# Block 1 of a feed-forward up-projection: two weight sums written over the raw gate weights, and the gate vector of the feed-forward asked for in blocks 8 to 15

## The chip, the cores and the metric

The kernel runs on one core of a Trainium2 chip. The metric is the device time of one execution in microseconds (us); lower is better. Engines: PE is TensorE (matrix products), DVE is VectorE, ACT is ScalarE, POOL is GpSimd, and SP is SyncE, whose queue issues most of the DMAs.

## What is computed

One layer of a diffusion transformer on 1024 positions of width 1024, all in fp32: a Hyena mixer, then a convolutional feed-forward with 2816 hidden channels. The change lies in the feed-forward. Cut to what matters:

```python
def conv_ffn(u, w_up, conv_w, conv_b, w_down, rows, cols):
    a, g = jnp.split(u @ w_up, 2, axis=-1)
    g = grid_dwconv(g, conv_w, conv_b, rows, cols)      # 3 x 3, depthwise, on a 16 x 64 grid
    return (jax.nn.silu(g) * a) @ w_down

sh1, sc1, g1, sh2, sc2, g2 = adaln_params(c, mod_w, mod_b)
x = x + g1 * hyena_mix(modulate(rmsnorm(x, norm_g[0]), sh1, sc1), hy_params)
x = x + g2 * conv_ffn(modulate(rmsnorm(x, norm_g[1]), sh2, sc2), *ffn_p, rows, 64)
return rmsnorm(x, final_g)
```

`g2` is the gate vector: one sixth (piece 5) of the product of `silu(c)` with `mod_w`. It is used only after the down-projection has begun to give results.

## The kernel before

Every fp32 product is made of three fp32r products: each operand is split into a high part (a copy by ACT, `..h`) and a low part (source minus high part, by DVE or POOL, `..l`), and `mm3` (L57 to L59) issues three matmuls.

The up-projection (`ffn_up`) runs over 22 blocks of 128 hidden channels. A block needs 128 columns of gate weights `g` and 128 of value weights `a`, 128 x 1024 each, which `up_load` brings in (L933) into two buffers with the tag `raw`. Block 0 is an ordinary product (`up_half`, 96 matmuls). Blocks 1 to 21 use Strassen's scheme in Winograd's form: 7 products of 12 matmuls each, 84 a block, from the quarters A11, A12 (in `g`), A22 (in `a`) and the sums S1 to S4 of them, against the same sums T1 to T4 of the activations. `up_prep(b)` makes the weights' operands: gh and gl from `g`; S1 and S2 in `s12` (POOL, L973 and L974), S3 and S4 in `s43` (POOL, L975 and L976); then the high and low parts (L962 and L963). `s12` lies in buffer x2 and `s43` in x3, but block 1's `s12` lies in another tile (`junk`).

Buffers x0 to x3 hold the tiles `braw` until then: the quarters B11 and B21 of the activations, from which `self.tsum` makes T1 to T4 (DVE subtractions L912, splits L62 and L63, the tiles tT1 to tT4). Block 1 is prepared, in program order, ahead of `tsum`; its `s43` has to wait until braw3 is no longer read.

In a block, PE runs S1 into the bank `uz`, S2 into `s`; ACT copies both into `pu` (L1065, L1067); then S4 goes on top of `uz`, which DVE adds into the convolution's padded tile (L1073), and S3 on top of `s`, which DVE adds into `at` (L1075); then comes the first product of the next block, and then A22 by T4 on top of the same `s`, once L1075 has read it. `up_tail` runs the convolution of the block before: one ACT instruction (L1005) and eight on DVE (`facc`, L1010), the SiLU (L1012), the product (L1013) and the store (L1014).

The gate vector is made by the generator `mod_gen(5)`: eight steps, each a DMA of 512 KB into the one buffer `mw` (L282) and one DVE instruction over 128 x 1024 (`macc`, L284 or L286); the last step also adds a bias (L308), and sums over the partitions on PE (four matmuls, L312). `ffn_up` asks for one step at the end of each block from 2 on, so in blocks 2 to 9.

The order of the instructions on each engine isn't the order of the program alone. A scheduler of the framework fixes it when the kernel is built: position in the program is priority, and an instruction of low priority goes ahead wherever, by the scheduler's own model of time, its engine has nothing ready of higher priority. On the chip each engine then runs its own list strictly in that order. SP's queue does too.

Of the kernel before, what the change touches and what calls it, by code (L numbers as in the profile page):

```python
# [13 lines left out]
ALU = mybir.AluOpType  # L14
# [4 lines left out]
D = 1024  # L19
# [28 lines left out]
class Kern:  # L48
# [903 lines left out]
    def up_prep(self, b):  # L952
        nc, op = self.nc, self.op
        if b >= NHT:
            return
        self.up_load(b)
        g, a = self.upraw.pop(b)
        lo, hi = slice(0, 512), slice(512, 1024)
        A = {}

        def hl(which, h, l, src, eng):
            nc.scalar.activation(out=h, in_=src, func=AF.Copy)  # L962
            eng.tensor_tensor(out=l, in0=src, in1=h.bitcast(F32), op=ALU.subtract)  # L963
            for i, w in enumerate(which):
                A[w] = h[:, i * 512:i * 512 + 512], l[:, i * 512:i * 512 + 512]

        gh = self.wp.tile([128, D], F32R, tag="wh", name=f"gh{b}", bufs=2)
        gl = self.wp.tile([128, D], F32R, tag="wl", name=f"gl{b}", bufs=2)
        hl(("A11", "A12"), gh, gl, g, nc.vector)
        s12 = self.xtile(2, [128, D], f"s12_{b}") if b > 1 else op.tile([128, D], F32, tag="junk", name="s12_1")  # L970
        s43 = self.xtile(3, [128, D], f"s43_{b}")
        tt = nc.gpsimd.tensor_tensor
        tt(out=s12[:, lo], in0=a[:, lo], in1=a[:, hi], op=ALU.add)  # L973
        tt(out=s12[:, hi], in0=s12[:, lo], in1=g[:, lo], op=ALU.subtract)  # L974
        tt(out=s43[:, hi], in0=g[:, lo], in1=a[:, lo], op=ALU.subtract)  # L975
        tt(out=s43[:, lo], in0=g[:, hi], in1=s12[:, hi], op=ALU.subtract)  # L976
        h, l = (op.tile([128, D], F32R, tag=f"xn{i}", name=f"s12{x}{b}") for i, x in enumerate("hl"))
        hl(("S1", "S2"), h, l, s12, nc.vector)
        h, l = (op.tile([128, D], F32R, tag=f"xn{2 + i}", name=f"s43{x}{b}") for i, x in enumerate("hl"))
        hl(("S4", "S3"), h, l, s43, nc.gpsimd)  # L980
        h, l = (op.tile([128, 512], F32R, tag=t, name=f"a22{x}{b}", bufs=2) for t, x in (("ot", "h"), ("nt", "l")))
        hl(("A22",), h, l, a[:, hi], nc.gpsimd)
        self.A[b] = A
# [33 lines left out]
    def ffn_up(self):  # L1017
        nc, op = self.nc, self.op
        pads = []
        for i in range(2):  # L1020
            p = op.tile([128, 1216], F32, name=f"fpad{i}", tag=f"fpad{i}")
            nc.gpsimd.memset(p, 0.0)
            pads.append(p[:, 0:18 * 66].rearrange("p (r c) -> p r c", r=18))
        s0, at, x = {}, {}, {}
        mods = self.mod_gen(5, None)
        at[0] = op.tile([128, D], F32, tag="macc", name="at0")

        def p1(b):
            s0[b] = self.bank("mm", f"s0_{b}")
            self.up_mm(b, s0[b], "A11", "11", True)  # L1030
            x[b] = self.bank("mm", f"ux{b}")
            nc.scalar.activation(out=x[b], in_=s0[b], func=AF.Copy)

        def p2(b):
            self.up_mm(b, x[b], "A12", "21")
            nc.scalar.activation(out=pads[b % 2][:, 1:9, 1:65], in_=x.pop(b).rearrange("p (r c) -> p r c", r=8), func=AF.Copy)

        def p4(b):
            self.up_mm(b, s0[b], "A22", "T4")
            nc.scalar.activation(out=at[b][:, 0:512], in_=s0.pop(b), func=AF.Copy)  # L1040

        self.up_half(pads[0], at[0], 0)
        self.up_prep(1)
        p1(1)
        p2(1)
        for k in sorted(self.tsum):
            self.tsum[k]()
        self.up_half(pads[0], at[0], 1)
        for b in range(1, NHT + 1):
            if b < NHT:  # L1050
                self.up_prep(b + 1)
                if b > 1:
                    p1(b)
            if b > 1:
                p4(b - 1)
            self.up_tail(b - 1, pads[(b - 1) % 2], at.pop(b - 1))
            if b == NHT:
                break
            pad = pads[b % 2]
            z = self.bank("mm", f"uz{b}")  # L1060
            pu = op.tile([128, 2, 512], F32, tag="junk", name=f"pu{b}")
            p5, u2 = pu[:, 0], pu[:, 1]
            at[b] = self.xtile(1, [128, D], f"at{b}") if b % 2 else op.tile([128, D], F32, tag="macc", name=f"at{b}")
            self.up_mm(b, z, "S1", "T1", True)
            nc.scalar.activation(out=p5, in_=z, func=AF.Copy)  # L1065
            self.up_mm(b, s0[b], "S2", "T2")
            nc.scalar.activation(out=u2, in_=s0[b], func=AF.Copy)  # L1067
            if b == NHT - 1:
                self.down_start()
            if b > 1:  # L1070
                p2(b)
            self.up_mm(b, z, "S4", "22")
            nc.vector.tensor_tensor(out=pad[:, 9:17, 1:65], in0=z.rearrange("p (r c) -> p r c", r=8), in1=u2.rearrange("p (r c) -> p r c", r=8), op=ALU.add)  # L1073
            self.up_mm(b, s0[b], "S3", "T3")
            nc.vector.tensor_tensor(out=at[b][:, 512:1024], in0=s0[b], in1=p5, op=ALU.add)  # L1075
            if b >= 2:
                next(mods, None)

    def down_start(self):
# [395 lines left out]
```

## Time and profile before

| | us |
|---|---|
| median of 3 executions | 1323.33 |
| lowest, highest | 1321.83, 1326.72 |
| the profiled execution | 1323.98 |
| its span, first to last instruction | 1321.9 |
| PE busy in the span | 1241.8 |
| DVE busy in the span | 1071.6 |
| POOL busy in the span | 405.9 |

Times in the rows are us from the start of the span. PE's clock is given as a share of full speed: 1.0 is 2.4 GHz and half of it 1.2 GHz. The up-projection runs from about 606 us to about 1065 us of the span, and block 1 from about 637 us to 680 us. The stretch is read first by busy time, then by what PE waited for, then instruction by instruction.

### The profile page before, as it was taken

Reading aid. Unit: us, or ns where it says so; the run is one execution under the profiler, and the core shown is the slowest. Engines: PE = TensorE matmul, PEld = TensorE weight load, DVE = VectorE, ACT = ScalarE, POOL = GpSimd, SP = SyncE. Lnnn points to the kernel's source line nnn. Section 1 sums busy time; section 2 is a strip of 40 time slices with the busy share of each in tenths; the row PEclk is TensorE's granted clock in tenths of the full one; section 3 lists DMA queues with packets and bytes.
Section 4 is the critical chain, followed back from the end, with each engine's and each line's share of the span. In section 5 each row is a group of like instructions: output and inputs, shape, how many; then the busy total and the mean of one; then the engine's idle time right before and its main releaser. Section 6 shows DMA issues by size and latency. Waiting matters only on the chain. (4 is left out here: it accounts for less than half of the span.)

```text
span 1321.9 us, 16127 instructions
## 1 busy us (share of the span) xinstructions
PE 1241.8 (94%) x5368; PEld 976.2 (74%) x5368; DVE 1071.6 (81%) x1353; ACT 745.9 (56%) x1221; POOL 405.9 (31%) x317
## 2 busy tenths in 40 slices
PE   7999999999899999999989899999999999988976
PEld 1687768777677767888767778888888878866854
DVE  7899875578686998795989998788888797866897
ACT  4798865677676879463644434444444454325343
POOL 2000011012100210000276446455555303724872
PEclk9999989999899999999989989999999999999988
DMA  9555689989989997544033431222222388568932
GB/s 339 179 157 153 213 276 281 272 241 261 262 255 298 273 294 263 175 143 175 15 106 99 149 127 66 95 80 85 75 96 81 127 291 297 176 198 267 340 103 95
DMA packets 114416, 247.12 MB, mean 187 GB/s; under 512 B 12660, under 2 KB 25844, under 8 KB 114334
## 3 DMA queue, kind: packets, MB, share of 16 engines
q1 hardware_dynamic: 98806, 232.60, 54.0%
q0 software_dynamic: 14848, 13.39, 5.0%
q8 instruction: 42, 0.69, 0.2%
q14 instruction: 40, 0.33, 0.1%
q10 hardware_dynamic: 680, 0.12, 0.0%
HBM read 192.05 MB, written 54.00 MB: 186 GB/s over the span
## 5 line engine op out<-in xcount | busy, mean ns | idle before, releaser
L1010 DVE SCALAR_TENSOR_TENSOR facc<-fpad,v_ffn_conv_w,facc 128x1024 f32<-128x1024 f32 x176 | 225.8, 1286 | 23.0 <-ACT facc L1005 19.4
L63 DVE TENSOR_TENSOR dl<-dr,dh 128x512 fp32r<-128x512 f32 x132 | 109.1, 871 | 11.6 <-ACT dh L62 10.5
L62 ACT ACTIVATE dh<-dr 128x512 fp32r<-128x512 f32 x132 | 76.2, 626 | 72.7 <-issue 15.8
L507 POOL DMA_DIRECT2D k_b<-in_k_b_dram x64 | 33.8, 530 | 269.0 <-PE ks L59 188.0
L973 POOL TENSOR_TENSOR s<-wrua 128x512 f32<-128x512 f32 x21 | 37.4, 1782 | 187.5 <-DVE s12l L963 101.7
L57 PE MATMUL dA<-dh,dh 128*128 128x512 f32 x176 | 70.1, 398 | 12.8 <-ACT u2macc L1310 7.7
L58 PE MATMUL dA<-dl,dh 128*128 128x512 f32 x176 | 69.6, 396 | 3.2 <-DVE dl L63 3.2
L963 POOL TENSOR_TENSOR s43l<-s,s43h 128x1024 fp32r<-128x1024 f32 x21 | 50.3, 2396 | 65.1 <-ACT s43h L962 65.1
L59 PE MATMUL dA<-dh,dl 128*128 128x512 f32 x176 | 68.9, 393 | 0.0
L58 PE MATMUL dB<-dl,dh 128*128 128x512 f32 x132 | 52.5, 397 | 7.2 <-DVE dl L63 7.1
L57 PE MATMUL dB<-dh,dh 128*128 128x512 f32 x132 | 52.0, 394 | 0.2 <-ACT dh L62 0.2
L59 PE MATMUL dB<-dh,dl 128*128 128x512 f32 x132 | 52.1, 395 | 0.0
L1005 ACT ACTIVATE facc<-fpad,v_ffn_conv_b,v_ffn_conv_w 128x1024 f32<-128x1024 f32 x22 | 26.6, 1209 | 44.2 <-DVE fpad L1073 44.2
L58 PE MATMUL op<-wlo,qh 128*128 128x512 f32 x128 | 50.2, 392 | 0.0
L57 PEld LDWEIGHTS dA<-dh,dh 128*128 128x128 f32 x176 | 33.5, 190 | 22.4 <-ACT u2macc L1310 8.1
L57 PE MATMUL op<-who,qh 128*128 128x512 f32 x128 | 49.9, 393 | 0.0
L59 PE MATMUL op<-who,ql 128*128 128x512 f32 x128 | 49.9, 390 | 0.0
L507 POOL DMA_DIRECT2D k_bi<-in_k_bi_dram x32 | 17.1, 534 | 104.6 <-PE zd L59 47.9
L286 DVE SCALAR_TENSOR_TENSOR macc<-mw,scl,macc 128x1024 f32<-128x1024 f32 x28 | 38.1, 1362 | 9.8 <-DMA mw<-in_mod_w_dram 9.6
L63 DVE TENSOR_TENSOR wlin<-wrin,whin 128x1024 fp32r<-128x1024 f32 x24 | 29.3, 1221 | 19.6 <-ACT whin L62 18.2
L962 ACT ACTIVATE s12h<-s 128x1024 fp32r<-128x1024 f32 x21 | 22.3, 1061 | 40.5 <-PE s L58 36.2
L573 ACT ACTIVATE who<-wro,invn 128x512 fp32r<-128x512 f32 x32 | 21.8, 718 | 37.1 <-PE op L59 28.5
(617 smaller groups left out, 4131.8 us busy)
## 6 DMA issues: line engine op xcount, KB each, us to landing
dr<-in_ffn_w_down_dram SPq DMA_DIRECT2D x77, 256.0 KB, 5.6
mw<-in_mod_w_dram SPq DMA_DIRECT2D x32, 512.0 KB, 4.8
dr<-du SPq DMA_DIRECT2D x55, 256.0 KB, 4.3
wrin<-in_hy_w_in_dram SPq DMA_DIRECT2D x24, 512.0 KB, 6.7
wrug<-in_ffn_w_up_dram SPq DMA_DIRECT2D x22, 512.0 KB, 3.5
wrua<-in_ffn_w_up_dram SPq DMA_DIRECT2D x22, 512.0 KB, 4.5
du<-fs SPq DMA_DIRECT2D x22, 512.0 KB, 2.6
dr<-du SPq DMA_DIRECT2D x22, 512.0 KB, 5.2
```

Of the source, the lines that this page charges most:

```text
L57: mm(out=out, lhsT=lh, rhs=rh, start=start, stop=False, **kw)
L58: mm(out=out, lhsT=lh, rhs=rl, start=False, stop=False, **kw)
L59: mm(out=out, lhsT=ll, rhs=rh, start=False, stop=stop, **kw)
L62: self.nc.scalar.activation(out=hi, in_=src, func=AF.Copy)
L63: self.nc.vector.tensor_tensor(out=lo, in0=src, in1=hi.bitcast(F32), op=ALU.subtract)
L286: nc.vector.scalar_tensor_tensor(out=acc, in0=w, scalar=self.scl[:, kt:kt + 1], in1=acc, op0=ALU.mult, op1=ALU.add)
L507: self.nc.gpsimd.dma_start(out=b, in_=self.a[name][k2])
L962: nc.scalar.activation(out=h, in_=src, func=AF.Copy)
L963: eng.tensor_tensor(out=l, in0=src, in1=h.bitcast(F32), op=ALU.subtract)
L973: tt(out=s12[:, lo], in0=a[:, lo], in1=a[:, hi], op=ALU.add)
L1005: nc.scalar.activation(out=av, in_=pad[:, 1:17, 1:65], func=AF.Identity, scale=self.cw[:, b, 4:5], bias=self.cb[:, b:b + 1])
L1010: nc.vector.scalar_tensor_tensor(out=av, in0=pad[:, dy:dy + 16, dx:dx + 64], scalar=self.cw[:, b, i:i + 1], in1=av, op0=ALU.mult, op1=ALU.add)
```

## The change

Two edits. In block 1 alone, `s43` is no longer a tile of its own in x3 but the raw gate weights' tile `g`, so that S3 and S4 overwrite it. For that the two halves of `s43` change places in every block: S3 now stands in the low half and S4 in the high one, so that L975 overwrites only columns that nothing reads after it. And `ffn_up` asks for the steps of `mod_gen(5)` from block 8 on, which are blocks 8 to 15.

```diff
-        s43 = self.xtile(3, [128, D], f"s43_{b}")
+        s43 = self.xtile(3, [128, D], f"s43_{b}") if b > 1 else g
         tt = nc.gpsimd.tensor_tensor
         tt(out=s12[:, lo], in0=a[:, lo], in1=a[:, hi], op=ALU.add)
         tt(out=s12[:, hi], in0=s12[:, lo], in1=g[:, lo], op=ALU.subtract)
-        tt(out=s43[:, hi], in0=g[:, lo], in1=a[:, lo], op=ALU.subtract)
-        tt(out=s43[:, lo], in0=g[:, hi], in1=s12[:, hi], op=ALU.subtract)
+        tt(out=s43[:, lo], in0=g[:, lo], in1=a[:, lo], op=ALU.subtract)
+        tt(out=s43[:, hi], in0=g[:, hi], in1=s12[:, hi], op=ALU.subtract)
...
-        hl(("S4", "S3"), h, l, s43, nc.gpsimd)
+        hl(("S3", "S4"), h, l, s43, nc.gpsimd)
...
             self.up_mm(b, s0[b], "S3", "T3")
             nc.vector.tensor_tensor(out=at[b][:, 512:1024], in0=s0[b], in1=p5, op=ALU.add)
-            if b >= 2:
+            if b >= 8:
                 next(mods, None)
```

## Rows read from the trace of the kernel before

**Rows 1.** Busy time by stretch: us, each engine's busy time, PE's clock, DMA.
```profile
640.00:660.00 20.00, 18.74 (x83) 15.21 (x82) 20.00 (x34) 13.58 (x23) 3.74 (x1) 1.00 0.04 5
660.00:672.00 12.00, 5.59 (x16) 3.90 (x15) 8.00 (x8) 4.64 (x7) 9.54 (x6) 0.72 0.39 124
700.00:720.00 20.00, 18.61 (x83) 15.10 (x82) 19.93 (x18) 8.89 (x12) 10.58 (x6) 1.00 0.38 131
880.00:900.00 20.00, 20.00 (x90) 16.57 (x89) 16.65 (x15) 9.15 (x12) 11.47 (x7) 1.00 0.23 79
```
**Rows 2.** What PE waited for, 655 to 1130 us: total, times, longest.
```profile
PE s L57 <- DVE at L1075: 6.3, 4, 2.7
```
**Rows 3.** Timeline of PE, end of block 1: start, duration [idle before it <- releaser].
```profile
660.08 0.39 PE L59 MATMUL s<-tT2h,s12l 128*128 128x512 f32 x1
666.88 0.79 PE L57 MATMUL uz<-b22hl,s43h 128*128 128x512 f32 x1 [6.41 <-ACT pu L1065]
671.90 0.39 PE L57 MATMUL s<-tT3h,s43h 128*128 128x512 f32 x1
```
**Rows 4.** Timeline of ACT in block 1.
```profile
640.20 1.07 ACT L962 ACTIVATE s12h<-s 128x1024 fp32r<-128x1024 f32 x1
657.12 1.14 ACT L62 ACTIVATE tT4h<-braw 128x512 fp32r<-128x512 f32 x2
664.25 1.06 ACT L962 ACTIVATE s43h<-s 128x1024 fp32r<-128x1024 f32 x1 [5.98 <-POOL s L976]
666.25 0.57 ACT L1065 ACTIVATE pu<-uz 128x512 f32<-128x512 f32 x1
```
**Rows 5.** Timeline of POOL in block 1.
```profile
628.71 1.29 POOL L974 TENSOR_TENSOR s<-s,wrug 128x512 f32<-128x512 f32 x1
656.26 5.51 POOL L963 TENSOR_TENSOR a22l<-wrua,a22h 128x512 fp32r<-128x512 f32 x1 [26.27 <-ACT a22h L962]
661.74 1.25 POOL L975 TENSOR_TENSOR s<-wrug,wrua 128x512 f32<-128x512 f32 x1
665.38 2.35 POOL L963 TENSOR_TENSOR s43l<-s,s43h 128x1024 fp32r<-128x1024 f32 x1 [1.17 <-ACT s43h L962]
```
**Rows 6.** Timeline of DVE in block 1.
```profile
659.37 1.29 DVE L912 TENSOR_TENSOR braw<-braw 128x512 f32<-128x512 f32 x2
665.85 3.03 DVE L63 TENSOR_TENSOR tT4l<-braw,tT4h 128x512 fp32r<-128x512 f32 x2 [4.00 <-ACT tT4h L62]
674.92 1.22 DVE L963 TENSOR_TENSOR s12l<-s,s12h 128x1024 fp32r<-128x1024 f32 x1 [1.74 <-ACT s12h L962]
```
**Rows 7.** Timeline of PE, the products A22 by T4 of blocks 1, 3, 4 and 5.
```profile
677.99 0.49 PE L57 MATMUL s<-tT4h,a22h 128*128 128x512 f32 x1 [0.47 <-DVE at L1075]
717.74 0.50 PE L57 MATMUL s<-tT4h,a22h 128*128 128x512 f32 x1 [1.40 <-DVE at L1075]
738.82 0.50 PE L57 MATMUL s<-tT4h,a22h 128*128 128x512 f32 x1 [1.76 <-DVE at L1075]
760.88 0.79 PE L57 MATMUL s<-tT4h,a22h 128*128 128x512 f32 x1 [2.71 <-DVE at L1075]
767.29 0.40 PE L57 MATMUL uz<-tT1h,s12h 128*128 128x512 f32 x1
```
**Rows 8.** Timeline of DVE, the gate vector's steps among blocks 2 to 5.
```profile
695.46 0.68 DVE L1075 TENSOR_TENSOR at<-s,pu 128x512 f32<-128x512 f32 x1
697.25 2.42 DVE L284 TENSOR_SCALAR macc<-mw,scl 128x1024 f32<-128x1024 f32 x1
717.01 0.68 DVE L1075 TENSOR_TENSOR at<-s,pu 128x512 f32<-128x512 f32 x1
749.99 1.28 DVE L286 SCALAR_TENSOR_TENSOR macc<-mw,scl,macc 128x1024 f32<-128x1024 f32 x1 [2.84 <-DMA mw<-in_mod_w_dram]
```
**Rows 9.** Timeline of SP's queue.
```profile
664.24 0.33 SPq L933 DMA_DIRECT2D wrua<-in_ffn_w_up_dram  x1
771.10 0.33 SPq L1234 DMA_DIRECT2D fg<-in_final_g_dram  x1
```

## The prediction, made before the changed kernel was run

> **What bounds the kernel now.** I read busy time by stretch first. From about 780 us PE is full: 20.00 of 20 us, 90 matmuls, with DVE at 16.65 [rows 1]. There the up-projection runs at PE's pace, one matmul per 20.00/90 = 0.222 us, a block of 84 in 18.7 us. Between 640 and 760 us it is otherwise: DVE is full (20.00 and 19.93 of 20) and PE has gaps (18.74 and 18.61) [rows 1]. So the second view is what PE waited for: 6.3 us in four waits for DVE's L1075 [rows 2], and one wait of 6.41 us for ACT's copy L1065 in block 1 [rows 3].
>
> That one wait is worth following. PE ends S2 at 660.08 + 0.39 and starts S4 at 666.88 [rows 3]. L1065 itself needs only bank `uz`, full since S1 ended; it is late because ACT runs in order and stands at s43h, idle 5.98 us for POOL's S4 sum [rows 4]. POOL does S3 and S4 only from 661.74, since x3 is read by `tsum` and since a22l ahead of it took 5.51 us [rows 5]. Behind s43h on ACT stand the last two tT4h and then L1065 [rows 4, 6]; DVE stands idle 4.00 us for that same tT4h [rows 6]. In 660 to 672 us the granted clock is 0.72 in the mean [rows 1], so after the gap it is at the lower of its levels, 1.2 GHz, for a while: the 12 matmuls of S4 take 671.90 - 666.88 = 5.02 us, where 12 x 0.222 = 2.67 is full pace [rows 1, 3]. 2.35 us are lost so.
>
> The four waits for L1075 are 0.47, 1.40, 1.76 and 2.71 us, at the end of blocks 1, 3, 4 and 5 [rows 7]. After the last the matmul has the same 0.79 us as after block 1's gap, so the lower clock again: 15 matmuls from 760.88 to 767.29 take 6.41 us instead of 3.33, so 3.08 lost. Everything that can be won in this stretch is 6.41 + 2.35 + 6.34 + 3.08 = 18.2 us. Behind 780 us a shift is carried on unchanged, since PE is full, and the down-projection starts from the last blocks' results.
>
> **Edit 1, S3 and S4 over the raw gate weights.** It removes block 1's wait for x3. The sums can follow S2 on POOL, which ends at 630.0 [rows 5]; g's other readers in that block (gh, gl) are done by then. Two sums of 1.25 us, s43h behind s12h on ACT (641.3 to 642.3), s43l of 2.35 us on POOL [rows 4, 5]: ready at about 645, needed at 660.5. That is a cover of 15 us. If POOL were slowed there as a22l was (5.51 us for an instruction of half s43l's columns), s43l would take 11 us and end at 654, still in time. s43h costs ACT 1.06 us ahead of the copy into `ux`; ACT is busy 13.58 of 20 us [rows 1], so I cost it at nothing; with the cover gone it is 1.06.
>
> What is late next: L1065 behind the last two tT4h, whose source DVE gives at 659.37 + 1.29 = 660.66 [rows 6]. So tT4h ends at about 661.3, L1065 at 661.9, and S4 starts there: a gap of about 1.5 us, as long as those of 1.40 and 1.76 us after which the matmul rows return to 0.50 us at once [rows 7]. So no lower clock. The product A22 by T4 moves from 677.99 to 661.9 + 24 x 0.222 (S4, S3) + 2.67 (next block's first product) = 669.9 if DVE follows: 8.1 us at most.
>
> DVE follows only by what it stood idle, as it is full to 740 us. It stood 4.00 us for tT4h and 1.74 for s12h of block 2 [rows 6]: 5.7 us. The second hangs on the loads. g's buffer is now held until s43l (645 rather than 664.2), but wrua's goes free with a22l at 661.77 rather than after L975, so it can be issued at 661.8 instead of 664.24 [rows 5, 9]; some 2.4 us sooner, which covers the 1.74. From the other side: POOL's three instructions (1.25 + 1.25 + 2.35) move from a stretch where DVE waited into one where it is full. In its old place s43l made two tT4l take 3.03 us; 1.29 is what two such instructions take [rows 6]. So DVE wins back 1.74 there and pays between 0 and 4.85 in the new place. I take 1.9, near the old price. Edit 1 on DVE's path: 4.00 + 1.74 + 1.74 - 1.9 = 5.6 us, bounds 2.6 and 7.5. PE gains more (up to 8.1) and gives the surplus back at the later waits for L1075.
>
> The Trainium skill, in "SBUF — State Buffer", section "Who interferes with whom", has a rule against this edit: a DVE instruction with two SBUF inputs and a GpSimd instruction that reads SBUF exclude each other, and the later one waits for the whole of the other. By that rule the sum would be taken with the full 4.85 us. The rows agree that the two engines lengthen one another, but 5.51 us on POOL came without a lengthened DVE instruction beside it, so which side pays isn't settled here.
>
> Edit 1's exchange of the halves changes no instruction's size: nothing.
>
> **Edit 2, the gate vector asked for later.** Among blocks 2 to 5, seven steps stand on DVE; the first takes 2.42 us, others 1.28, and the sixth also idles 2.84 us for its load [rows 8]. Blocks take DVE 717.01 - 695.46 = 21.55 us there, against PE's 18.7 to 19. Were all seven gone from the stretch, the three waits in blocks 3 to 5 (5.87) and the lower clock (3.08) would go: 8.95 us. But I don't think they go. The scheduler runs an instruction of low priority wherever its model finds the engine free: the load of `fg`, written behind the whole up-projection, is issued at 771.10, when its buffer comes free [rows 9]. And the first step stands right behind block 2's L1075, where it was asked for, but in the middle of the convolution of block 1, which has higher priority [rows 8]: a chain of dependent instructions leaves places that any ready instruction takes. With the later request the steps still find these places; only a second convolution that is ready at the same time now goes ahead of them. I expect each step about one place later, so that one step of 1.27 to 2.42 us fewer stands ahead of the L1075 of blocks 3, 4 and 5. I take 1.8. The bounds are 0 and 8.95. The four matmuls for the vector (L312), with the two copies behind them, move on PE from block 9 to about block 15, where PE is just as full: nothing; the loads ahead use a queue that is mostly idle.
>
> **The sum.** 5.6 + 1.8 = 7.4 us off the profiled execution of 1323.98 (a span of 1321.9 and 2.1 around it): 1316.6. That execution lies 0.65 above the median of 1323.33, so the forecast for the median is 1316.0.
>
> **The rivals.** (a) The steps really go to blocks 8 to 15. For it: there DVE has 3.35 us free in 20 [rows 1], and a scheduler that sees DVE full would hold them back; against it: `fg`. Then of the 18.2 us only block 1's gap of 1.5 and about 1 elsewhere remain: 15.7 off, 1308. (b) DVE gives edit 1 back: it pays 4.85 for POOL's moved instructions, or L1075 of block 1 stands in DVE's order behind s12l of block 2, which hangs on the load at 661.8. Then 2.6 to 4 us are left: 1320. (c) The s43 operands aren't used earlier because ACT's order keeps s43h behind the last splits: no change, 1323. (d) Slower: the steps stand in DVE's order ahead of L1075 in blocks where their load isn't there yet. One such wait was 2.84 us and led to 2.71 + 3.08 = 5.8 us on PE [rows 7, 8]. One is in the time already; the gain of 7.4 is used up from the second further one on, and with three PE loses 17.4 against 7.4: 1333. Against it: in blocks 8 to 15 the steps' period of a block leaves the load about 17 us.
>
> **How the numbers follow.** Forecast, spread 1313 to 1319: 0.50. (a), spread 1305 to 1312: 0.24. (b), 1317 to 1322: 0.14. (c): 0.05. (d): 0.07. The range of 80%: from the middle of (a) to the upper part of (b), 1307 to 1321; its lower end also holds edit 1's upper bound. A difference of 0.5%, 6.6 us, is about what a measurement here can tell from none; the line is at 1316.7. Of the forecast's 0.50 a little over 0.30 lies below it, with (a): faster 0.55. Same: the rest of it, (b) and (c): 0.38. Slower: (d), 0.07.
>
> **What would show it.** Right: s43h on ACT before 650 us; PE's gap before S4 under 2.5 us with the matmuls after it at 0.39 to 0.50 us; A22 by T4 of block 1 at 670 to 673; `macc` still between 695 and 775 us; the waits for L1075 in blocks 3 to 5 near 5 us in sum. Wrong: a gap of over 4 us before S4; a long wait for L1075 already in block 1; `macc` after 800 us (then the time is that of (a)); new waits for L1075 in blocks 8 to 15.

## The result and the profile after

The change makes the kernel slower by 0.56%: the ratio is 1.0056, with a 95% interval of 1.0037 to 1.0074. The medians are 1330.14 us in 20 executions, and 1322.18 us for the kernel before in as many on the same chip. The forecast was 1316.0 and its range 1307 to 1321, so sign and range are both missed. The profiled execution took 1333.56 us with a span of 1331.5 us.

The stretches of busy time, read as [rows 1] (us, busy time and instructions of PE, PE's weight loads, DVE, ACT and POOL, PE's clock, DMA share, GB/s); the second fence is the kernel before in the first of these stretches, which the prediction did not look at:

```profile
600.00:640.00 40.00, 37.41 (x167) 30.48 (x166) 26.22 (x39) 16.73 (x28) 5.53 (x4) 0.91 0.33 119
660.00:680.00 20.00, 11.04 (x34) 8.20 (x33) 12.87 (x14) 6.28 (x11) 12.75 (x6) 0.76 0.31 105
740.00:760.00 20.00, 15.81 (x58) 12.48 (x57) 17.26 (x16) 6.86 (x9) 9.81 (x6) 0.83 0.46 150
880.00:900.00 20.00, 20.00 (x90) 16.57 (x89) 16.68 (x15) 9.61 (x12) 10.51 (x6) 1.00 0.24 79
```

```profile
600.00:640.00 40.00, 38.45 (x184) 31.22 (x183) 26.23 (x41) 18.67 (x32) 2.57 (x2) 1.00 0.33 120
```

PE is still full at 880 us, so what the up-projection lost was lost earlier: the clock is now 0.91 already in 600 to 640 us, where it was 1.00, and 660 to 680 and 740 to 760 us still have holes.

What PE waited for between 600 and 1040 us (total, times, longest), against [rows 2]:

```profile
PE uz L57 <- ACT pu L1065: 6.9, 1, 6.9
PE s L57 <- DVE at L1075: 4.5, 2, 4.2
PE n21p L384 <- DVE xn L377: 2.4, 1, 2.4
PE s L57 <- ACT pu L1067: 2.0, 1, 2.0
PE ux L57 <- ACT ux L1032: 1.7, 1, 1.7
```

The wait that the change was to shorten, 6.41 us in [rows 3], is 6.9 us, and a new one for L1067 stands behind it. The waits for L1075 fell from 6.3 to 4.5 us. The end of block 1 on PE and ACT, and the next block, as [rows 3, 4, 7]:

```profile
669.76 0.80 PE L57 MATMUL uz<-b22hl,s43h 128*128 128x512 f32 x1 [6.92 <-ACT pu L1065]
676.76 0.50 PE L57 MATMUL s<-tT3h,s43h 128*128 128x512 f32 x1 [2.04 <-ACT pu L1067]
746.34 0.79 PE L57 MATMUL s<-tT4h,a22h 128*128 128x512 f32 x1 [4.19 <-DVE at L1075]
```

```profile
642.02 1.07 ACT L962 ACTIVATE s43h<-wrug 128x1024 fp32r<-128x1024 f32 x1
668.59 0.63 ACT L962 ACTIVATE a22h<-wrua 128x512 fp32r<-128x512 f32 x1 [6.63 <-DMA wrua<-in_ffn_w_up_dram]
669.13 0.58 ACT L1065 ACTIVATE pu<-uz 128x512 f32<-128x512 f32 x1
669.61 1.14 ACT L62 ACTIVATE tT4h<-braw 128x512 fp32r<-128x512 f32 x2
675.17 1.06 ACT L962 ACTIVATE s12h<-s 128x1024 fp32r<-128x1024 f32 x1 [4.43 <-POOL s L974]
676.13 0.58 ACT L1067 ACTIVATE pu<-s 128x512 f32<-128x512 f32 x1
```

s43h is at 642.02, right behind s12h, and waits for nothing, as forecast. But ACT's list is another one. Before, L1065 and L1067 stood at once behind the last tT4h, and the splits of block 2 (gh, a22h, s12h) behind them. Now a22h of block 2 stands ahead of L1065, and waits 6.63 us for its weights; the last two tT4h stand behind L1065; and s12h of block 2 stands ahead of L1067, and waits 4.43 us for POOL. ACT was idle ahead of L1065 about as long as before (6.63 us instead of 5.98), only for something else. One more place has changed, at the start of block 1: s43h and the last of the splits b22hl now stand between s12h and the copy into `ux` (L1032), which starts 2.41 us behind s12h's start instead of 0.95.

POOL (the second of the moved sums, s43l, a22l), SP's queue and DVE, as [rows 5, 9, 6]:

```profile
629.32 1.72 POOL L976 TENSOR_TENSOR wrug<-wrug,s 128x512 f32<-128x512 f32 x1
643.16 2.53 POOL L963 TENSOR_TENSOR s43l<-wrug,s43h 128x1024 fp32r<-128x1024 f32 x1 [12.13 <-ACT s43h L962]
657.82 7.00 POOL L963 TENSOR_TENSOR a22l<-wrua,a22h 128x512 fp32r<-128x512 f32 x1 [12.13 <-ACT a22h L962]
```

```profile
664.85 0.33 SPq L933 DMA_DIRECT2D wrua<-in_ffn_w_up_dram  x1
```

```profile
628.26 4.65 DVE L377 TENSOR_SCALAR xn<-x1o,n21r 128x1024 f32<-128x1024 f32 x4
643.37 2.87 DVE L912 TENSOR_TENSOR braw<-b,braw 128x512 f32<-128x512 f32 x1
670.26 1.52 DVE L63 TENSOR_TENSOR tT4l<-braw,tT4h 128x512 fp32r<-128x512 f32 x1 [6.55 <-ACT tT4h L62]
```

The load that a22h waits for is issued at 664.85, when a22l of block 1 lets go of the buffer (657.82 + 7.00). DVE stands idle 6.55 us for tT4h where it stood 4.00. And POOL's moved work is paid on DVE: the four L377 beside the two sums take 4.65 us, and one L912 beside s43l takes 2.87 where an undisturbed one takes 0.68. In the kernel before the same four L377 are

```profile
630.25 2.74 DVE L377 TENSOR_SCALAR xn<-x1o,n21r 128x1024 f32<-128x1024 f32 x4
```

The gate vector's steps on DVE, as [rows 8]:

```profile
703.92 0.68 DVE L1075 TENSOR_TENSOR at<-s,pu 128x512 f32<-128x512 f32 x1
709.23 0.84 DVE L284 TENSOR_SCALAR macc<-mw,scl 128x1024 f32<-128x1024 f32 x1
720.48 0.68 DVE L1075 TENSOR_TENSOR at<-s,pu 128x512 f32<-128x512 f32 x1
736.63 1.28 DVE L286 SCALAR_TENSOR_TENSOR macc<-mw,scl,macc 128x1024 f32<-128x1024 f32 x1 [2.69 <-DMA mw<-in_mod_w_dram]
745.61 0.68 DVE L1075 TENSOR_TENSOR at<-s,pu 128x512 f32<-128x512 f32 x1
757.29 1.28 DVE L286 SCALAR_TENSOR_TENSOR macc<-mw,scl,macc 128x1024 f32<-128x1024 f32 x1 [2.63 <-DMA mw<-in_mod_w_dram]
770.70 1.97 DVE L286 SCALAR_TENSOR_TENSOR macc<-mw,scl,macc 128x1024 f32<-128x1024 f32 x1
```

The first step stands one place later, 5.31 us behind the start of block 2's L1075 instead of 1.79, and the next two are later too; the other five stand where they stood, the last 3.24 us behind the start of block 5's L1075 (3.22 before). All eight are still in blocks 3 to 6: asking in blocks 8 to 15 didn't bring them there. Between the L1075 of blocks 2 and 3 there is one step fewer, between those of 3 and 4 one more, and DVE now idles for two loads of `mw`, 2.69 + 2.63 us, instead of 2.84 + 0.19.

**Time by stretch.** To compare kernels I cut the span by four marks that every kernel has: ACT's gh of block 1 (L962), and the first matmul of the product S1 in blocks 1, 8 and 21.

| us | gh of block 1 | S1 of block 1 | S1 of 8 | S1 of 21 | span |
|---|---|---|---|---|---|
| before | 621.61 | 654.87 | 804.96 | 1054.21 | 1321.9 |
| after | 619.62 | 657.24 | 809.17 | 1058.42 | 1331.5 |

Times in two traces are compared from such a mark, since the spans are shifted against each other. A is the time from the first mark to the second (33.26 before, 37.62 after), B from there to the third (150.09, 151.93), C to the fourth (249.25 in both). What lies ahead of the first mark took 611.9 to 625.8 us in the traces of this study, and what lies behind the last 265.4 to 273.2, both without regard to the edits: two traces of the kernel after gave 273.1 and 269.5 for the latter, two of the kernel before 267.7 and 269.7. So a single trace's span says little, and the 273.1 behind the first matmul of block 21's S1 in the profiled execution can't be put down to the change. A, B and C can be compared.

| kernel | A | B | C | sum against before | measured ratio |
|---|---|---|---|---|---|
| before, two traces | 33.26, 33.24 | 150.09, 147.42 | 249.25 | 0 | 1 |
| after, two traces | 37.62, 39.20 | 151.93, 151.42 | 249.25 | +8.1 | 1.0056 |
| edit 1 alone | 39.08 | 151.23 | 249.25 | +8.3 | 1.0074 |
| edit 2 alone | 33.24 | 150.45 | 249.25 | +1.7 | 1.0030 |
| a22h of block 2 behind L1065 | 39.09 | 150.60 | 249.26 | +7.7 | 1.0069 |
| POOL kept from DVE | 36.47 | 152.82 | 249.26 | +7.3 | 1.0060 |
| POOL kept from DVE, a22h and a22l of block 2 behind L1067 | 36.50 | 152.15 | 249.25 | +6.6 | 1.0044 |
| a22l on DVE | 37.24 | 149.14 | 249.25 | +4.4 | 1.0045 |
| gate steps held to 8 to 15 | 33.28 | 143.14 | 265.12 | +10.3 | 1.0094 |
| the same, behind L1073 | 33.25 | 142.92 | 249.91 | -5.2 | 0.9955 |
| that, and a22l on DVE | 33.25 | 141.15 | 249.91 | -6.9 | 0.9965 |
| that, and edit 1 mended | 33.41 | 138.02 | 249.90 | -9.9 | 0.9922 |

The fifth column is A + B + C less the mean of the two traces of before, 431.26 us. B differs by 2.67 us between those two, so 2 or 3 us of a sum are the trace's own. Nearly all of the 2.67 lies in block 5 (from S1 to S1 24.48 and 21.88 us): in the second trace of before its wait for L1075 has the full clock behind it, where the first had the lower one.

```profile
755.16 0.50 PE L57 MATMUL s<-tT4h,a22h 128*128 128x512 f32 x1 [2.55 <-DVE at L1075]
```

A ratio of 0.001 is 1.3 us, and in every line the sum lies in the interval measured, or within 0.1 us of it. The slowdown is A + B: +5.2 in A, +2.9 in B. Counted from S1 to S1, block 1 takes 26.72 us after and 25.96 before, so the stretch that the change was made for neither won nor lost much; block 4 takes 25.96 instead of 21.11, and block 5 19.46 instead of 24.48.

### The profile page after: what moved, and what is told of

Read it like the earlier page. It is cut to its first block, busy times and chain, and to the rows that moved or that the text cites. A ratio compares the mean times of both kernels' runs of the same rounds, so it can differ in the third digit from the quotient of the medians.

```text
span 1331.5 us, 16129 instructions
## 1 busy us (share of the span) xinstructions
PE 1250.5 (94%) x5368; PEld 982.9 (74%) x5368; DVE 1079.3 (81%) x1353; ACT 746.5 (56%) x1221; POOL 401.5 (30%) x317
## 5 line engine op out<-in xcount | busy, mean ns | idle before, releaser
L63 DVE TENSOR_TENSOR dl<-dr,dh 128x512 fp32r<-128x512 f32 x132 | 112.9, 904 | 9.2 <-ACT dh L62 7.3
L962 ACT ACTIVATE s12h<-s 128x1024 fp32r<-128x1024 f32 x21 | 22.3, 1061 | 40.6 <-PE s L58 36.2
L974 POOL TENSOR_TENSOR s<-s,wrug 128x512 f32<-128x512 f32 x21 | 42.8, 2039 | 1.6
L58 PEld LDWEIGHTS dA<-dl,dh 128*128 128x128 f32 x176 | 34.6, 196 | 11.0 <-DVE dl L63 4.0
```

The costliest lines, as they stand in the source:

```text
L58: mm(out=out, lhsT=lh, rhs=rl, start=False, stop=False, **kw)
L63: self.nc.vector.tensor_tensor(out=lo, in0=src, in1=hi.bitcast(F32), op=ALU.subtract)
```

## The experiments

Each ratio is against the kernel before on the same chip. Inserted lines shift line numbers, and a row below has those of its own kernel; the text says which line of the kernel after (or before) it is. Of each edit only the lines that matter are shown; remarks behind # are mine.

**Edit 1 alone.**

```diff
-            if b >= 8:
+            if b >= 2:
                 next(mods, None)
```

> Edit 1 alone (block 1's S3 and S4 over the raw gate weights; gate vector asked for in blocks 2 to 9 as before). Theory A, edit 1 costs the time: ACT stands at a22h of block 2, waiting for the weights' load, ahead of L1065, so PE still waits 6 to 7 us before S4 of block 1, and POOL's moved instructions lengthen DVE's work by 1.9 us at L377 and 2.2 us at L912; time 1326 to 1331, as the changed kernel. Theory B, edit 2 costs it: 1320 to 1323, as before. Theory C, the excess lies in the down-projection and comes with neither edit as such: the start of the down-projection within 1 us of before, the time anywhere in 1318 to 1332.

1.0074 (1.0052 to 1.0096). The wait before S4 is there without edit 2, and so is ACT's wait ahead of it:

```profile
665.52 0.79 PE L57 MATMUL uz<-b22hl,s43h 128*128 128x512 f32 x1 [5.18 <-ACT pu L1065]
```

```profile
664.35 0.63 ACT L962 ACTIVATE a22h<-wrua 128x512 fp32r<-128x512 f32 x1 [6.50 <-DMA wrua<-in_ffn_w_up_dram]
```

So theory A holds (the median was 1328.82): edit 1 by itself accounts for the whole slowdown.

**Edit 2 alone.** The kernel before, with

```diff
-            if b >= 2:
+            if b >= 8:
                 next(mods, None)
```

> Edit 2 alone (gate vector asked for from block 8 on; S3 and S4 of block 1 in x3 as before). Theory A: the eight steps still run within blocks 3 to 6, about 8 us later; time within 3 us of before, 1319 to 1324. Theory B, edit 2 costs the time: 1327 to 1331, with waits for L1075 of more than 6.3 us in sum.

1.0030 (1.0013 to 1.0046): slightly slower, by about 4 us where theory A has at most 3. The steps run in blocks 3 to 6 again, a step idles for its load, and the next L1075 is late:

```profile
728.73 1.28 DVE L286 SCALAR_TENSOR_TENSOR macc<-mw,scl,macc 128x1024 f32<-128x1024 f32 x1 [3.07 <-DMA mw<-in_mod_w_dram]
```

```profile
738.42 0.80 PE L57 MATMUL s<-tT4h,a22h 128*128 128x512 f32 x1 [6.17 <-DVE at L1075]
```

The waits for L1075 are 8.2 us in all, against 6.3 [rows 2]. The two edits' own prices don't add up: with edit 1 beside it, edit 2 adds nothing that the stretches show. Why that is so stays open.

**The split a22h of block 2 behind L1065.** The kernel after, with a22h and a22l of block 2 queued behind block 1's copy into p5:

```diff
+            c5 = nc.scalar.activation(out=p5, in_=z, func=AF.Copy)
+            if b == 1:
+                with self.tc.issue_after(c5.ins):
+                    self.a22()          # up_prep(2) leaves it out
```

> The changed kernel, but a22h and a22l of block 2 are put behind L1065 (the copy of S1 into pu) of block 1 on ACT. Theory A: PE's wait before S4 falls from 6.9 us to 2 us or less, the matmuls after it are at full clock, and DVE's wait for tT4h (6.6 us) falls below 2; time 4 to 8 us less than the changed kernel, 1322 to 1326. Rival: DVE or the load of block 2's weights is late next and the wait moves to the next product; within 2 us of the changed kernel, 1328 to 1332.

1.0069 (1.0050 to 1.0089): no gain. L1065 (L1072 in this kernel) is early now, at 663.37, and the wait has moved one product on, to S3 and L1067 (L1077):

```profile
677.77 0.80 PE L57 MATMUL s<-tT3h,s43h 128*128 128x512 f32 x1 [9.11 <-ACT pu L1077]
```

```profile
671.73 0.63 ACT L962 ACTIVATE a22h<-wrua 128x512 fp32r<-128x512 f32 x1 [7.07 <-DMA wrua<-in_ffn_w_up_dram]
677.14 0.58 ACT L1077 ACTIVATE pu<-s 128x512 f32<-128x512 f32 x1
```

So it isn't the place of this one instruction: a22h still waits for the load, now behind L1065, and it and s12h of block 2 stand ahead of L1067. The rival holds: the wait moves to the next product.

**POOL's moved work kept from DVE.** The kernel after; S3's and S4's sums of block 1 wait for the last of the four L377, and s43l of block 1 is DVE's:

```diff
+        if b == 1:
+            for i in (s3, s4):          # the sums L975, L976
+                self.tc.add_manual_dep(i.ins, self.xlast.ins.name, ...)
-        hl(("S3", "S4"), h, l, s43, nc.gpsimd)
+        hl(("S3", "S4"), h, l, s43, nc.gpsimd if b > 1 else nc.vector)
```

> The changed kernel, but POOL's S3 and S4 sums of block 1 wait until DVE's four L377 are done, and s43l of block 1 is made by DVE. Theory: POOL's moved instructions lengthened DVE's (four L377 4.65 us instead of 2.74, one L912 2.87 instead of 0.68), and these lie on the way to the T sums. Then the stretch from gh of block 1 to S1 of block 1, 33.26 us before and 37.62 in the changed kernel, falls to 33.3 to 34.6. Rival: the stretch is longer because ACT has s43h ahead of the copy into ux; then it stays at 36 to 38. Whole time 2 to 5 us less than the changed kernel in the first case, within 2 us in the second.

1.0060 (1.0032 to 1.0089). That POOL lengthens the four L377 is confirmed, since they are back at 2.74 us. But A falls only to 36.47, which is the rival's 36 to 38 and not the 33.3 to 34.6 of the theory, and B loses again what A won. S4 no longer waits; S3 waits 9.80 us for L1067 (L1070), which stands behind a22h and s12h of block 2. What is left of A is seen on PE at the copy into `ux` (L1032, here L1035), which stands behind s43h and a split b22hl on ACT:

```profile
638.51 0.50 PE L57 MATMUL ux<-bh,gh 128*128 128x512 f32 x1 [2.88 <-ACT ux L1035]
671.28 0.80 PE L57 MATMUL s<-tT3h,s43h 128*128 128x512 f32 x1 [9.80 <-ACT pu L1070]
```

**Both, with a22h and a22l of block 2 behind L1067.**

> The changed kernel with both suspected costs of edit 1 taken out: POOL's S3 and S4 of block 1 behind DVE's L377 and s43l of block 1 on DVE, and a22h and a22l of block 2 behind L1067 of block 1. If these two are the whole cost: the stretch from gh to S1 of block 1 33.3 to 34.6 us, the wait before S4 at most 2.5 us with full clock after it, S1 of block 1 to S1 of block 8 143 to 147 us (150.1 before); 3 to 7 us less than the kernel before, 10 less than the changed one. Rival: DVE's arrears decide, and what PE wins in block 1 comes back as waits for L1075 in blocks 2 to 6: within 3 us of the kernel before.

1.0044 (1.0020 to 1.0067), slower than either forecast. PE's waits for L1065 and L1067 are gone (that for the copy into `ux`, 2.88 us, is not), and PE waits 8.81 us for L1075 (L1088) instead. L1088 stands on DVE behind s12l of block 2, as rival (b) of the prediction has it, and s12l hangs on the same load, which is issued at 661.65:

```profile
675.07 0.80 PE L57 MATMUL s<-tT4h,a22h 128*128 128x512 f32 x1 [8.81 <-DVE at L1088]
```

```profile
670.12 1.31 DVE L963 TENSOR_TENSOR s12l<-s,s12h 128x1024 fp32r<-128x1024 f32 x1 [9.65 <-ACT s12h L962]
```

**a22l of block 1 on DVE.** The kernel after, so that the buffer comes free sooner:

```diff
-        hl(("A22",), h, l, a[:, hi], nc.gpsimd)
+        hl(("A22",), h, l, a[:, hi], nc.gpsimd if b > 1 else nc.vector)
```

> The changed kernel, one thing different: a22l of block 1 is made by DVE instead of POOL. Theory: block 1's value weights are held until a22l has read them (POOL took 7.00 us for it while DVE made the T sums), so block 2's are loaded late (664.85), and a22h, s12h and s12l of block 2, which wait for them, hold up L1065, L1067 and L1075 of block 1. Then the load is issued 5 to 7 us sooner in the stretch, the wait before S4 is 2 us or less, S1 of block 1 to S1 of block 8 takes 144 to 148 us (151.9 in the changed kernel), and the time is 4 to 8 us less than the changed kernel. Rival: POOL's slowness isn't the cause and the load is as late as before; within 2 us of the changed kernel.

1.0045 (1.0025 to 1.0064). The load is issued at 654.98, which is 38.9 us behind gh of block 1 instead of 45.2, so 6.3 us sooner, and the wait before S4 is gone. B falls to 149.14, short of the 144 to 148 of the theory: S3 waits for L1067, which stands behind s12h of block 2, and that now waits for POOL rather than for the load.

```profile
654.98 0.33 SPq L933 DMA_DIRECT2D wrua<-in_ffn_w_up_dram  x1
```

```profile
667.52 1.06 ACT L962 ACTIVATE s12h<-s 128x1024 fp32r<-128x1024 f32 x1 [6.48 <-POOL s L974]
```

```profile
669.12 0.79 PE L57 MATMUL s<-tT3h,s43h 128*128 128x512 f32 x1 [7.48 <-ACT pu L1067]
```

POOL's sum L975 of block 2 took 5.19 us here, beside a full DVE.

**The gate steps really in blocks 8 to 15.** The kernel before; each step's DVE instruction is queued behind L1075 of its block:

```diff
-            if b >= 2:
-                next(mods, None)
+            if b >= 8:
+                with self.tc.issue_after(i75.ins):   # i75: L1075
+                    next(mods, None)
```

> The kernel before, with the gate vector's steps really in blocks 8 to 15: each step's DVE instruction is queued behind L1075 of its block. If the steps are what makes the L1075 of blocks 3 to 5 late: these waits (5.87 us) and the lower clock behind the last (3.08) go, and no wait comes in blocks 8 to 15; 1322.2 - 8.95 = 1313, taken as 1312 to 1317. If DVE's arrears from the T sums alone make them late: 1320 to 1323.

1.0094 (1.0066 to 1.0121), slower than either forecast. B falls to 143.14, as rival (a) has it, and C rises by 15.87 us. From S1 to S1, blocks 10 to 14 take 20.14 us each rather than 19.04 (5 x 1.10 = 5.5). The block with the sums over partitions, 20.77 us in the kernel before, takes 31.06: PE waits there 3.47 us for L1075 and 2.95 for `macc`. DVE in one of the blocks before it:

```profile
882.12 1.29 DVE L1010 SCALAR_TENSOR_TENSOR facc<-fpad,v_ffn_conv_w,facc 128x1024 f32<-128x1024 f32 x1 [1.34 <-ACT facc L1005]
883.31 0.68 DVE L1075 TENSOR_TENSOR at<-s,pu 128x512 f32<-128x512 f32 x1
883.91 2.69 DVE L286 SCALAR_TENSOR_TENSOR macc<-mw,scl,macc 128x1024 f32<-128x1024 f32 x1
```

The step takes 2.69 us; it starts 0.77 us after POOL's s43l, which began at 883.14 and took 2.38, and so do its neighbours in the other blocks (2.67 to 2.69). And DVE's free time isn't behind L1075: 1.34 us of it lie ahead of the convolution's first `facc`.

**The same, in the hole.** Each step goes right behind L1073, where DVE then waits for ACT anyway, and the last part (bias, sums on PE) comes a block later:

```diff
+            if b >= 8:
+                with self.tc.issue_after(i73.ins):   # i73: L1073
+                    next(mods, None)
...
             if kt == KT - 1:
+                if ch == 5:
+                    yield 1
```

> The kernel before, with the gate vector's steps in blocks 8 to 15, each DVE instruction queued right behind L1073 of its block, where DVE stands idle 1.34 us for ACT's L1005 in every block, and the bias and PE's sums a block later. If the place decides: blocks 1 to 8 are 7 us shorter as with the steps behind L1075, and blocks 8 to 15 keep 19.04 us each; 5 to 9 us less than the kernel before on the same chip, ratio 0.993 to 0.996. If any step in these blocks costs time: 20.1 us a block there, 1 us or more above the kernel before.

0.9955 (0.9935 to 0.9975): 1313.08 us, faster than either kernel. L1073 is L1075 in this kernel:

```profile
900.40 0.69 DVE L1075 TENSOR_TENSOR fpad<-uz,pu 128x512 f32<-128x512 f32 x1
901.01 1.71 DVE L286 SCALAR_TENSOR_TENSOR macc<-mw,scl,macc 128x1024 f32<-128x1024 f32 x1
902.64 1.28 DVE L1012 SCALAR_TENSOR_TENSOR facc<-fpad,v_ffn_conv_w,facc 128x1024 f32<-128x1024 f32 x1
```

The `facc` behind the step waits for nothing any more, the blocks stay at 19.04 us, and only block 16, with the sums, takes 21.43. So the same eight steps in the same blocks, with the sums a block later, make 6 us less than the kernel before instead of 12 us more. Of the 15.2 us between the two in C, about 5.5 are the place of the steps in DVE's list (blocks 10 to 14); the rest lies in the block with the sums, where the place of the last step and the later sums were changed together and can't be told apart.

**With edit 1 mended as well, and with a22l alone.** To the last kernel, one run adds edit 1 with all the repairs: the sums behind L377, s43l and a22l of block 1 on DVE, and s43h of block 1 queued behind the copy into `ux`. Another adds only a22l of block 1 on DVE, with `s43` in x3 as before.

```diff
-            nc.scalar.activation(out=x[b], in_=s0[b], func=AF.Copy)
+            cx = nc.scalar.activation(out=x[b], in_=s0[b], func=AF.Copy)
+            if b == 1:
+                with self.tc.issue_after(cx.ins):
+                    self.s34()          # s43h and s43l, on ACT and DVE
```

> Both edits in a form that takes out what was found: S3 and S4 of block 1 over the raw gate weights, but their sums behind DVE's L377, s43l and a22l of block 1 on DVE and s43h behind the copy into ux; the gate vector's steps in blocks 8 to 15 right behind L1073. If edit 1 is worth anything once these are gone: from gh of block 1 to S1 of block 1 33.3 to 34.5 us and from S1 of block 1 to S1 of block 8 136 to 141 us, 8 to 13 us less than the kernel before, ratio 0.990 to 0.994. If DVE's arrears take it back: 142 to 144 us for the latter and a ratio of 0.995 to 0.997, as with the gate steps alone.

> The kernel before with the gate vector's steps in blocks 8 to 15 right behind L1073, and a22l of block 1 on DVE; S3 and S4 of block 1 stay in x3. If POOL's slow a22l (5.51 us) is what holds the S3 and S4 sums up, the wait before S4 falls from 6.4 to 2 to 4 us, without edit 1; S1 of block 1 to S1 of block 8 138 to 141 us, ratio to the kernel before 0.991 to 0.994. If x3 holds them up: 142.5 to 143.5 us and 0.995 to 0.996.

The first: 0.9922 (0.9893 to 0.9952), 1308.93 us, the fastest kernel here. A is back at 33.41 and B at 138.02, both as its first forecast has them. ACT has the two copies (L1065 and L1067, here L1080 and L1082) where PE wants them, and what is left of the gap is 3.25 us at the next block's start, with the lower clock soon behind it (granted 0.57 from 666 to 670 us):

```profile
649.49 0.60 ACT L1080 ACTIVATE pu<-uz 128x512 f32<-128x512 f32 x1
652.51 0.58 ACT L1082 ACTIVATE pu<-s 128x512 f32<-128x512 f32 x1
```

```profile
665.24 0.47 PE L57 MATMUL uz<-tT1h,s12h 128*128 128x512 f32 x1 [3.25 <-DVE fpad L1088]
```

The second: 0.9965 (0.9944 to 0.9987), 1313.64 us. The wait before S4 stays, 5.79 us, and POOL's S3 sum (L975, here L977) now waits for a split tT4l, which reads `braw`:

```profile
670.40 0.79 PE L57 MATMUL uz<-b22hl,s43h 128*128 128x512 f32 x1 [5.79 <-ACT pu L1067]
```

```profile
663.07 3.45 POOL L977 TENSOR_TENSOR s<-wrug,wrua 128x512 f32<-128x512 f32 x1 [28.92 <-DVE tT4l L63]
```

So x3 holds the sums up, and a22l on DVE by itself isn't what helps (B is 141.15, between its two forecasts, and the ratio no better than without it). Edit 1 with all its repairs is worth 1313.64 - 1308.93 = 4.7 us in the medians of 12 and 6 executions; the means differ by 5.2, with a 95% interval of 1.5 to 8.9. Which of the repairs is worth how much inside B was not taken apart.

**Before and after once more.** A copy of each, one execution (1317.17 us before, 1324.54 after), for a second trace.

> The kernel before, unchanged, a second trace of it: how far two executions of one program differ by stretch. The down-projection (first to last matmul) took 243.0 us in the first trace of before and 246.1 to 248.5 in five changed kernels whose PE, POOL and SP orders there are the same. If that length belongs to the kernels, it is 242 to 244 here; if it varies by execution, it may come out at 245 to 249. The stretch from gh of block 1 to S1 should be 33.3 and the up-projection after it 399.3, both within 0.3.

> The changed kernel, unchanged, a second trace of it: how far two executions of it differ by stretch. If the cost of the change lies where the first trace puts it: from gh of block 1 to S1 of block 1 37 to 39 us (33.25 in each trace of before), a wait of 5 to 7 us before S4 that ends with L1065, and S1 of block 1 to S1 of block 8 150 to 153 us (150.1 and 147.4 in the two traces of before). If the down-projection belongs to the change it is 248 us again; if it varies by execution, as in the two traces of before (243.0 and 245.0), it may be anywhere from 241 to 249.

They give the second numbers of the table. In the second trace of before, A is as expected; B + C is 396.67 us and not 399.3, by block 5's clock. The second trace of after has the same waits before S4 and S3, 5.21 and 2.60 us, and before a later A22 by T4, 4.52; its A is 39.20, just above the 37 to 39 expected. So the mechanism doesn't hang on one execution.

## Why the prediction was wrong, and where it was right

**Right: what bounds the kernel.** Late in the up-projection a shift is only carried along: C, from about 805 us on, is 249.25 or 249.26 in every kernel whose gate steps run before block 8. (A block takes 19.04 us there, 0.227 a matmul, and not the 18.7 that I read from a count of 90.) The gap before S4 did come from x3, as the run with only a22l on DVE shows, and s43h came early once x3 was out of the way, right behind s12h. The lower clock after the gap costs what I said: the 12 matmuls of S4 take 676.76 - 2.04 - 669.76 = 4.96 us, against 5.02 before. Of the 8.1 us that the stretches lost, 5.2 lie in A, where I had put nothing on PE's path, and 2.9 in B, where I had a gain.

**Wrong: the step "what is late next" of edit 1.** It followed the list of the kernel before, with one instruction taken out, to L1065 at 661.9. But the list itself is made anew, and in the new one a22h and s12h of block 2 stand ahead of block 1's two copies. Why the scheduler put them there (its model no longer has s43h's wait, and sees another time for block 2's operands) is my inference; that it did is seen in both traces of after and in that of edit 1 alone. I had written that wrua could be issued at 661.8, some 2.4 us sooner than before. Counted from gh of block 1 it was issued at 45.2 us, where before it was at 42.6: A had grown, and a22l took 7.00 us and not the 5.51 of [rows 5]. (Nor was L975 what the old load waited for: 664.24 is when L976 ends, 662.96 + 1.25.) The gap of 1.5 us that I forecast was 6.92 + 2.04 us, and the 5.7 us that DVE was to win back were lost again (6.55 us idle for one tT4h). The page of the kernel before shows nothing of such an exchange of places, but a rival was owed: an instruction of block 2 ahead of L1065 on ACT, as rival (b) has one on DVE.

**Mis-sized: POOL's moved instructions, taken at 1.9 us on DVE.** Measured are 4.65 - 2.74 = 1.91 on the L377 and 2.87 - 0.68 = 2.19 on L912, 4.1 in all, and with no return: the 1.74 us were not won in the old place either, where the last two tT4l now stand beside POOL's work for block 2 and take 1.52 + 1.76 = 3.28 us, against 3.03 before. Nor did I ask what stands beside the moved sums. It is the L377 that PE's transposes (n21p) wait for: 2.45 us instead of 1.55, and the granted clock behind it is 0.50 from 630 to 635 us, where it was 1.00. The Trainium skill, in "SBUF — State Buffer", section "Who interferes with whom", counts operations of L377's kind (`tensor_scalar`) among those that can take the ports that DVE shares with GpSimd, and lets whichever is first hold them for its whole instruction. The traces agree: beside POOL 4.65 us, without it 2.74. By that rule the sum would have had 4.85 in place of 1.9, near the 4.1 measured.

**Wrong: s43h ahead of the copy into `ux` "at nothing".** I read ACT's 13.58 us of 20 as cover. The copy is on PE's way, and in the new list a split b22hl went ahead of it together with s43h. The wait for it grew from 1.26 us to 1.68 and 2.37 in the two traces of after, where PE itself came late, and to 2.88 in the run where POOL was kept from DVE. There the wait is 1.62 us longer, and the 12 matmuls behind it take 4.45 us instead of 2.86 (granted clock 0.75 from 640 to 645 us). Together these are 3.21 us, all by which that run's A of 36.47 exceeds the 33.26 of before. Where s43h stands behind the copy A is 33.41. So the changed places ahead of the copy are worth about 3 us, three times the 1.06 named as the price without cover. A busy share doesn't say whether one instruction has someone waiting behind it.

**Edit 2: the place right, the sign wrong.** The first three steps did go about one place later, and all stayed in blocks 3 to 6, as argued from `fg`. But "one step fewer ahead of the L1075 of blocks 3, 4 and 5" holds for block 3 alone; block 4 got one more. Two of the steps now wait for their loads, 5.3 us instead of 3.0, which is rival (d)'s mechanism in small; the first of these loads is issued only at 730.29, 5.1 us after the step before it has ended, behind a store (729.00) and the load of wrua (729.87) on SP's queue. Alone the edit costs 0.30%. The expected 1.8 us weren't there.

**Rival (a).** Its gain is real: B is 4.3 to 7.2 us shorter when the steps leave blocks 2 to 5 (143.1 and 142.9 against 150.1 and 147.4), less than the 8.95 priced. 3.08 of that price were the lower clock behind block 5's wait, which the second trace of before doesn't have. Its premise was wrong, that DVE's 3.35 free us in 20 would take them at no cost. Behind L1075 a step costs its block 1.10 us (blocks 10 to 14), and the sums' block takes 10.3 more; behind L1073, with the sums a block later, the steps cost nothing and the sums' block takes 0.66 more.

**What stays open.** Why edit 2 adds nothing beside edit 1; which of the repairs cures B; and how A's rise divides between POOL's collision and the places ahead of the copy into `ux`: without the collision A is 36.5 instead of 37.2 to 39.2, and the collision without the changed places was not run. The spread of 2 us goes with the clock behind that copy. In the traces with 37.2 and 37.6 PE waits 1.94 and 1.68 us for it and the matmuls stay at the full clock; in those with 39.1 to 39.2 it waits 2.19 to 2.73 us and the lower clock follows.

## What to carry to other kernels

Where a scheduler makes each engine's list, an edit that takes away one wait gives a new list: ask which instruction of the next stage may now stand ahead of the ones that PE wants, and what it waits for. Free time on an in-order engine has a place: here a gate step cost nothing in the hole that a wait left, and 1.10 us a block a few instructions later. And when a buffer gets a second use, follow the next load of its neighbour back to the instruction that lets go of it; here getting that load 6 us sooner was by itself not enough, since other instructions of the next block still stood ahead of the copies.

## What the runs showed of the hardware

A POOL subtraction of 128x512 takes 1.25 to 1.30 us alone. Begun beside a DVE that ran without a break through tensor_tensor instructions with both inputs in SBUF, it took 5.51 us (a22l, kernel before), 7.00 (after), 7.17 (POOL kept from DVE) and 5.19 (L975, with a22l on DVE), and it ended 1.1 to 1.2 us after that run of DVE's ended. While a22l took 7.00, from 657.82 to 664.82, DVE's instructions over 128x512 kept their 0.68 us each until DVE ran out of work at 663.70. In the other direction one DVE instruction that started just behind a POOL instruction took 2.69 instead of 1.28 us, and one took 2.87 instead of 0.68. So in these traces POOL lost where DVE ran without a break, and DVE lost where POOL got in first. But the convolution's `facc` instructions, whose sum lies in PSUM, and POOL's subtractions don't lengthen one another: from 686.30 to 690.10 us of the kernel after DVE is busy 3.80 us of 3.80 with them and POOL 3.79, and POOL's three take 1.29 us each.
